# Hymba layer: value stores ahead of the inverse's loads, inverse and scan earlier in the matmul mix, second head's loads behind the scan, leading tile in mid-group

## The chip, the core and the metric

The kernel runs on one core of a Trainium2 chip. The metric is device time in microseconds (us), the median of three runs. The engines are PE (TensorE: matmuls and transposes into PSUM banks), DVE (VectorE), ACT (ScalarE), POOL (GpSimd) and SP (SyncE, which issues most DMAs, in the order of its queue).

## The reference, cut to what matters

One layer with two head groups side by side on T = 16 meta + 1024 tokens, D = 1024, all in fp32:

```
u        = rmsnorm(x);  p = u @ w_in            # one projection, split by columns
group 1: gated DeltaNet, 4 heads of 128, chunked: causal conv on q, k, v; per chunk
         solve (I + A) [U W] = rhs (A strictly lower triangular); then the scan over chunks
           v_new = U - W S;  o = (q e^g) S + (q k^T decay) v_new;  S = S e^g + k^T v_new
         o = rmsnorm(o) * w * silu(z)
group 2: forgetting attention, 8 heads of 64: logf = logsigmoid(f + b), c = cumsum(logf)
         softmax(q k^T / 8 + c_q - c_k, causal) v, in blocks of 128 queries
h   = x + concat(o1, o2) @ w_out
out = rmsnorm(h + swiglu(rmsnorm(h)))           # meta tokens dropped
```

## The kernel before, in words

**Precision.** A product in fp32 is made of three matmuls: each operand is split into a high and a low part (`split`: ACT casts the high part, DVE subtracts to get the low part, L163/L164 and L166/L167), and `mm3g` (L210) issues hi·hi, hi·lo, lo·hi. So each weight block that is loaded (`load_w`, raw_*, on SP's queue) costs one ACT and one DVE instruction (whi_*, wlo_*) before PE can use it, and each result that leaves a PSUM bank as an operand costs an ACT and a DVE instruction before the bank is free.

**What sets the order.** PE's order is written by the class `PeOrder` while the program is traced. It holds chains, which are generators that say when their next step is due, and one `fill`, a generator that is advanced by a matmul whenever no chain is due. `od.t` counts PE's time. The order on DVE, ACT, POOL and SP is set by the tile scheduler, which simulates the program; `tc.issue_after(x)` in the kernel makes an instruction wait in that order until x has been issued. Pools decide when a tile's space is free, and so which loads must wait.

**Stages around the change.** After the DeltaNet's projections:

- The *inverse* of the 64-wide triangular blocks: `invert_blocks` works on DVE (`up`, L527/L529, a chain of short instructions that begins when `ad` has been loaded, and ends with eight stores to `ud_d`, L549). Then `levels(hp)`, hp = 0, 1 for two pairs of heads, combines blocks by matmuls on PE. Each level's first step loads `ubk` (L599, 256 KB) and `na` (L601, two loads of 512 KB) on SP. They enter the mix by `od.add(levels(hp), LV0[hp] - 8.0)`, LV0 = (76, 119).
- The *fill* `fox()`: the attention's projections. First the gate z0, then values in two halves, fv1 (heads 4 to 7, with the forget gate's columns `fr`) and fv0 (heads 0 to 3), each in tiles −1 (16 meta tokens) and 0 to 7, then `fox_proj` for keys (fk) and queries (fq), four head pairs (0 to 3) in three chunks of tokens each (fq2_700 is pair 2's chunk at token 700). A value tile takes 24 matmuls. It leaves its bank by ACT, DVE and, in the first half, the copy to `fr` (L943), through `fvt`, which has three buffers, and is stored to DRAM in `v_d` (L940). A key or query chunk leaves through `fhl`, which has two buffers (ACT L768, DVE L769), and its store (L771, to `k_d` or `q_d`) is remembered in `last[0]`. `fox_load` (L710) loads the next weight block.
- After the levels the *scan* over eight chunks (L775 to L856), with `chunk_out` behind each chunk (`on` L868 on DVE, four transposes `ot` L874 on PE). The fill runs between its steps. What is left of the fill when the scan is done comes after it in one piece. Head 0's nine loads are issued in chunk 7.
- The *attention*: per head nine loads (`att_head`: `ka`, `qa`, `kk`, `sa`, `avt`), then scores (sc, L1009/L1010, sums `sm` on DVE L1014), transposes (pt), and values (po: L1075 for the meta tile by `phm` and `vm`, L1078/L1079 with the hi and lo parts `ph` and `pl`). Heads alternate between two pools: `ale` for even and `alo` for odd heads; `alo` is opened after the whole fill. `vm` holds the meta tokens' values, in eight copies of 16 rows; `vm_load` (L728) issues eight small loads per head, and head 1's call loads those of head 0 too. Head 1's loads were issued behind `last[0]`, the last store of q.
- While attention runs, its fill is the DeltaNet's half of the output projection, `wout_gdn`: tiles `wog` of 12 matmuls, each of which waits for a bank; DVE adds it to the residual `ht` (L1175), loaded from x on SP's queue while one head's loads have been issued, on POOL's queue once there are two. The fill starts `LD0` after a head's loads (10 us for the heads that lack time).
- After the heads: the attention's half of the output projection, the FFN (about half of the span) and the final norm. The change leaves them alone.

Of the kernel before, what the change touches and what calls it, by code (L numbers as in the profile page):

```python
# [9 lines left out]
F32 = mybir.dt.float32  # L10
F32R = mybir.dt.float32r
# [4 lines left out]
P = 128  # L16
# [13 lines left out]
GQ, GK, GV, GZ, FQ, FK, FV = 0, 512, 1024, 1536, 2056, 2568, 3080  # L30
TCH = ((0, 348), (348, 346), (694, 346))
GRP = 4
LV0 = (76.0, 119.0)
LAT = 0.4
ATT0 = 3.0
LEAD = 0.6
# [61 lines left out]
def tile_hymba_layer(ctx, tc, x, meta, attn_norm_w, w_in, conv_w, a_log, dt_bias, gdn_norm_w,  # L98
                     fgate_b, w_out, ffn_norm_w, w_gate, w_up, w_down, final_norm_w, out):
    nc = tc.nc  # L100
# [43 lines left out]
    rec_d = dram.tile([NT, P, 8, GH, P], F32, name="rec_d")  # L144
    ad_d = dram.tile([2, 4, 2, NT, 32, 32], F32, name="ad_d")
    ud_d = dram.tile([2, 4, 32, 2, NT, 32], F32, name="ud_d")
# [4 lines left out]
    v_d = dram.tile([FH, T, P], F32, name="v_d")  # L151
# [38 lines left out]
    def win_block(c0, n, name):  # L190
        ws = ([], [])
        for i in range(2):
            k0 = KT // 2 * i
            hl = load_w([(w_in_v[:, k0:k0 + KT // 2, c0:c0 + n], KT // 2 * n)], f"{name}_{i}")
            for o, t in zip(ws, hl):
                o.extend(t[:, n * k:n * k + n] for k in range(KT // 2))
        return ws
# [8 lines left out]
    od = PeOrder()  # L206
# [344 lines left out]
    for hp in range(2):  # L551
        c = 2 * P * hp
# [42 lines left out]
    def levels(hp):  # L595
        na = lp.tile([P, 2, NT, P], F32, tag="na", bufs=2, name=f"na_{hp}")
        tb = lp.tile([P, 2, NT, 32], F32, tag="tb", bufs=2, name=f"tb_{hp}")
        ubk = lp.tile([P, 2, NT, 32], F32, tag="ubk", bufs=2, name=f"ubk_{hp}")
        nc.sync.dma_start(ubk, ud_d[hp].rearrange("b j h t k -> (b j) h t k"))  # L599
        for i in range(2):  # L600
            nc.sync.dma_start(na[:, i], rec_d[:, :, 0, 2 * hp + i].rearrange("t p c -> p t c"))  # L601
        if not hp:
            lv_t["act"], lv_t["dve"] = tail[0]
        with tc.issue_after(lv_t["dve"].ins):
# [96 lines left out]
        yield from mm3g(acc[:rows, :n], [(uh[:, k, col:col + rows], ul[:, k, col:col + rows], w[0][k][:, :n],  # L701
                                          w[1][k][:, :n]) for k in range(KT)], n / 2400)

    last = [None]

    fox_ws = [(GZ, 256, "z0"), (FV + 256, 264, "fv1"), (FV, 256, "fv0"), (FK, 256, "fk0"), (FK + 256, 256, "fk1"),
              (FQ, 256, "fq0"), (FQ + 256, 256, "fq1")]
    fox_w = []

    def fox_load():  # L710
        if fox_ws:
            fox_w.append(win_block(*fox_ws.pop(0)))

    t_ld, hds, fixed, fq_m, h_ld = [], {}, [], [0], {}

    def att_tiles(i):
        ka = als[i].tile([NA + DH, T], F32R, name=f"ka{i}")
        qa = als[i].tile([NA + DH, S], F32R, name=f"qa{i}")
        nc.gpsimd.memset(ka[:NA].bitcast(F32), 1.0)
        nc.gpsimd.memset(qa[:NA].bitcast(F32), -1.0)  # L720
        fixed.append((ka, qa))

    NR = GRP * NM
    vms, pms = [], {}
# [194 lines left out]
    def fox():  # L919
        fox_load()  # L920
        w = fox_w.pop(0)
        for t in range(NT):
            if t == 1:
                fox_load()
            acc = ps_mm(f"z0_{t}")
            yield from proj_tmg(acc, t, w, 256)
            gate_out(t, acc, *((fvp, "fvt") if t < NT - 2 else (fp, "fhl")), 0)
        for b in (1, 0):
            n = 256 + 8 * b
            w = fox_w.pop(0)  # L930
            for t in range(-1, NT):
                if t == 1:
                    fox_load()
                col, rows = tok_cols(t)
                acc = (ps_mm if b or t % 2 else ps_t)(f"fv{b}_{t}")
                yield from proj_tmg(acc, t, w, n)
                vt = fvp.tile([P, 4, 2, DH], F32R, tag="fvt", name=f"fvt{b}_{t}")
                av = acc[:rows, :256].rearrange("p (h d) -> p h d", d=DH)
                split(vt[:rows, :, 0], vt[:rows, :, 1], av)
                nc.sync.dma_start(v_d[4 * b:4 * b + 4, col:col + rows].rearrange("h t d -> t h d"),  # L940
                                  vt[:rows].rearrange("p h a d -> p h (a d)").bitcast(F32))
                if b:
                    nc.vector.tensor_copy(fr[:rows, NT if t < 0 else t], acc[:rows, 256:264])  # L943
        fvc.close()
        yield from fox_proj(lambda m: k_d[m], TCH, 0, 1.0, "fk")
        od.add(csum(), od.t + 8.0)
        yield from fox_proj(lambda m: q_d[m].rearrange("a p c -> p a c"), ((NM, 342), (NM + 342, 342), (NM + 684, 340)), NM, -DH ** -0.5, "fq")

    lv_left, outs_left = {0, 1}, set(range(NT))
    for hp in range(2):  # L950
        od.add(levels(hp), LV0[hp] - 8.0)
    od.fill = fox()
    peo = ExitStack()
    peo.enter_context(tc.manual_schedule(engines={mybir.EngineType.PE}))
# [12 lines left out]
    od.add(scan(), od.t + 4.0, front=True)  # L967
    od.run(lambda: not outs_left)
    scc.close()
    while od.step_fill():  # L970
        pass
    uctx.close()

    alc = ExitStack()
    als.append(alc.enter_context(tc.tile_pool(name="alo", bufs=1)))
    atc = ExitStack()
    ap_ = atc.enter_context(tc.tile_pool(name="ap", bufs=1, side="right"))
    ap2 = atc.enter_context(tc.tile_pool(name="ap2", bufs=1, side="right"))
    rsum = ap_.tile([P, FH, NT], F32, name="rsum")
    for i in range(2):  # L980
        vms.append(ap2.tile([P, GRP, P], F32R, name=f"vm{i}"))
        nc.gpsimd.memset(vms[i].bitcast(F32), 0.0)
    att_tiles(1)
    masks = []

    def scores(h, g, hd, out):
# [54 lines left out]
    def values(h, g, hd, pts):  # L1041
        m, rows, vt = *hd[:2], hd[6]
        nk = GRP * (g + 1)
        nm = f"{g}_{h}"
        box = []
        for kt in (0, -1, *range(1, nk)):
            c0, j0 = NM + P * kt, max(0, kt - GRP * g)
            yield max(r for _, r in pts)
            pt = ps_t(f"pt_{nm}_{kt}")
            if kt < 0:  # L1050
                nc.tensor.transpose(pt[:NR, :P], pms.pop((h, g)), ident)
                od.pe(0.108)
            else:
                for j in range(j0, GRP):
                    nc.tensor.transpose(pt[:, P * j:P * j + P], pts[j][0][:, j, c0:c0 + P], ident)  # L1055
                    od.pe(0.108)
            q = slice(P * j0, 512)
            if kt < 0:
                ph = pl = ap2.tile([P, P], F32R, tag="phm", bufs=2, name=f"phm_{nm}")
                split(ph[:NR], ph[NR:], pt[:NR, :P])  # L1060
                meta_lo[0], meta_n[0] = tail[0][1], 0
            else:
                ph = ap2.tile([P, 512], F32R, tag="ph", bufs=3, name=f"ph_{nm}_{kt}")
                pl = ap2.tile([P, 512], F32R, tag="pl", bufs=3, name=f"pl_{nm}_{kt}")
                split(ph[:, q], pl[:, q], pt[:, q])
            nq = P if kt < 0 else 512 - P * j0
            rdy = od.on("dve", nq / 960 + 0.07, od.on("act", nq / 1200 + 0.06))

            def av(kt=kt, ph=ph, pl=pl, q=q):
                if kt == 0:  # L1070
                    box.append(ps_v(f"po_{nm}"))
                po = box[0]
                if kt < 0:
                    for j in range(GRP):
                        nc.tensor.matmul(po[:, P * j:P * j + P], vms[h % 2][:, j], ph, start=False, stop=False)  # L1075
                    od.pe(0.2135)
                    return
                nc.tensor.matmul(po[:, q], vt[:, kt], ph[:, q], start=kt == 0, stop=False)  # L1078
                nc.tensor.matmul(po[:, q], vt[:, kt], pl[:, q], start=False, stop=(kt == nk - 1))  # L1079
                od.pe((512 - q.start) / 1200)  # L1080
                if kt == nk - 1:
                    oa = ap2.tile([P, 512], F32, tag="oa", bufs=2, name=f"oa_{nm}")
                    nc.scalar.copy(oa, po)
                    od.on("act", 0.5)
                    for i in range(2):
                        last_o[0] = nc.gpsimd.dma_start(
                            o_d[GRP * g:GRP * g + GRP, rows, 4 * i + m].rearrange("t p c -> p t c"),
                            v3(oa[DH * i:DH * i + DH], GRP))

            avq.append((rdy, av))  # L1090
            yield from av_step(2)

    def attention():
        groups = [(h, g) for h in range(FH) for g in range(NT // GRP)]
        ptl, pos = {}, [0.0]

        def score_stream():
            for i, (h, g) in enumerate(groups):
                if h not in hds:
                    with tc.issue_after(last[0].ins) if h == 1 else nullcontext():  # L1100
                        hds[h] = att_head(h)
                ptl[i] = []
                for n, rdy in enumerate(scores(h, g, hds[h], ptl[i])):
                    pos[0] = i + n / (5, 9)[g]
                    yield max(rdy, t_ld[h] + LD0[i]) if i < len(LD0) else rdy
            pos[0] = 1e9

        ss = score_stream()

        def ahead(x):  # L1110
            while pos[0] < x:
                r = next(ss, None)
                if r is None:
                    return
                yield r

        yield from ahead(1.0)
        rot[0] = 0
        for i, (h, g) in enumerate(groups):
            nt = GRP * (g + 1) + 1  # L1120
            yield from ahead(i + 1.0)
            for k, rdy in enumerate(values(h, g, hds[h], ptl[i])):
                yield from ahead(i + 1.0 + LEAD + k / (2 * nt))
                yield rdy
        yield from av_step(0)
        rot[0] = 1
# [602 lines left out]
```

## Time and profile before

| | |
|---|---|
| median of 3 runs | 1305.55 us (1304.69 to 1306.87) |
| profiled execution | 1305.29 us, its span 1303.6 us, mean granted clock 0.996 |
| PE's idle time in the span, all waits | some 15 us, of which about 10 between 250 and 600 us |
| inverse's `ad` load issued | 233.03 us |
| fv1 on PE | 232.82 to 263.7 us |
| first chunk, last chunk of the scan | 375.49, 426.46 us |
| first wog tile | 439.26 us |
| attention's values | 463.5 to 590 us |

How to read it: PE is busy for nearly the whole span. A row of a timeline gives start, duration, engine, line, operation and out<-in, and in brackets how long the engine had been idle before it and what ended that. Matmuls are pipelined, so that their durations overlap; the distance between two starts is what a matmul takes of PE's time. `SPq` rows are DMA issues on SP's queue; they last as long as SP was held there.

### The profile page before, as it was taken

How to read it: one execution, taken by the hardware profiler on the slowest of the kernel's cores; microseconds unless marked ns; L12 is line 12 of the kernel's file. 1: busy time of each engine (PE TensorE's matmuls, PEld its weight loads, DVE VectorE, ACT ScalarE, POOL GpSimd, SP SyncE). 2: the span in 40 equal slices, each digit the busy share in tenths (PEclk: the TensorE clock that was granted, in tenths of full speed). 3: DMA queues.
4: the chain of work that ended last, by engine and by line, in shares of the span. 5: the costliest groups of instructions: out<-in, count | busy, mean ns of one | idle time of the engine just before them, and what ended most of it. 6: DMA issues, size and time to landing. Idle time of an engine off the chain costs nothing.

```text
span 1303.6 us, 20023 instructions
## 1 busy us (share of the span) xinstructions
PE 1281.6 (98%) x7434; PEld 1127.5 (86%) x7434; DVE 839.7 (64%) x1508; ACT 547.7 (42%) x940; POOL 348.8 (27%) x316
## 2 busy tenths in 40 slices
PE   9999999899999999999999999999999999999997
PEld 8999999899999888887778888888888888888886
DVE  6667898583246768886887666556666664365645
ACT  6455444142223557884553333233333343433332
POOL 2012213101022221112504534455334443020301
PEclk9999999999999999999999999999999999999999
DMA  6333625854389886737435644553444467945513
GB/s 230 99 118 110 183 86 141 234 143 154 127 285 304 220 236 190 183 94 253 168 114 161 198 165 155 186 163 129 159 155 166 165 212 268 393 178 197 207 64 129
DMA packets 185248, 232.07 MB, mean 178 GB/s; under 512 B 19816, under 2 KB 138176, under 8 KB 182336
## 3 DMA queue, kind: packets, MB, share of 16 engines
q1 hardware_dynamic: 182256, 222.15, 53.1%
q0 software_dynamic: 2896, 8.65, 2.2%
q8 instruction: 58, 0.95, 0.3%
q14 instruction: 38, 0.31, 0.1%
HBM read 153.11 MB, written 77.65 MB: 177 GB/s over the span
## 4 chain that ended last, share of the span: by engine, by line
PE 87%; DVE 5%; DMA 3%; issue 2%; SPq 1%; ACT 1%; POOL 0%; POOLq 0%; DVEq 0%; ACTq 0%
PE xp L1610 9%; PE yp L1610 7%; PE ua L1435 5%; PE ga L1435 5%; PE gb L1435 5%; PE ud L1435 5%; PE gd L1435 5%; PE ub L1435 5%; PE pj_fk L212 4%; PE pj_fq L212 3%; PE fv L212 3%; PE ue L1435 2%; PE ge L1435 2%; PE pt L1055 2%; PE wog L212 2%
## 5 line engine op out<-in xcount | busy, mean ns | idle before, releaser
L164 DVE TENSOR_TENSOR al_p<-ra_p,ah_p 128x2048 fp32r<-128x2048 f32 (+1 forms) x21 | 47.7, 2273 | 94.5 <-ACT ah_p L163 94.5
L163 ACT CAST ah_p<-ra_p 128x2048 fp32r<-128x2048 f32 (+1 forms) x21 | 37.1, 1767 | 106.2 <-PE xp L1610 47.9
L1610 PE MATMUL xp<-wl_p,ah_p 128*128 128x512 f32 (+1 forms) x176 | 67.3, 382 | 0.0
L1610 PE MATMUL xp<-wh_p,al_p 128*128 128x512 f32 (+1 forms) x176 | 67.3, 382 | 0.0
L1610 PE MATMUL xp<-wh_p,ah_p 128*128 128x512 f32 (+1 forms) x176 | 67.3, 382 | 0.0
L1491 POOL TENSOR_TENSOR gzw<-gzw,uzt 128x512 f32<-128x512 f32 x11 | 18.4, 1673 | 168.0 <-DVE uzt L1480 138.9
L1435 PE MATMUL gb<-uh_p,w_g_p 128*128 128x512 f32 x176 | 57.8, 389 | 0.0
L1435 PE MATMUL ub<-uh_p,w_u_p 128*128 128x512 f32 x176 | 57.7, 389 | 0.0
L1435 PE MATMUL gd<-uh_p,w_g_p 128*128 128x512 f32 x176 | 57.7, 389 | 0.0
L1435 PE MATMUL ud<-uh_p,w_u_p 128*128 128x512 f32 x176 | 57.7, 389 | 0.0
L163 ACT CAST ph<-pt 128x512 fp32r<-128x512 f32 (+1 forms) x96 | 45.2, 474 | 29.8 <-PE pt L1055 28.8
L164 DVE TENSOR_TENSOR pl<-pt,ph 128x512 fp32r<-128x512 f32 (+1 forms) x96 | 52.0, 554 | 8.4 <-ACT ph L163 7.8
L1491 POOL TENSOR_TENSOR gxy<-gxy,uxy 128x512 f32<-128x512 f32 x22 | 39.0, 1771 | 64.7 <-DVE uxy L1480 53.7
L164 DVE TENSOR_TENSOR w_u_p<-raw_u,w_u_p 128x512 fp32r<-128x512 f32 x42 | 41.9, 997 | 21.6 <-ACT w_u_p L163 21.5
L1019 ACT ACTIVATE pr<-pr,sm 128x144 f32<-128x144 f32 (+3 forms) x64 | 50.5, 791 | 10.0 <-DVE sm L1014 9.8
L1435 PE MATMUL ua<-uh_p,w_u_p 128*128 128x512 f32 x160 | 52.5, 389 | 0.0
L1435 PE MATMUL ga<-uh_p,w_g_p 128*128 128x512 f32 x160 | 52.5, 389 | 0.0
L1610 PE MATMUL yp<-wh_p,ah_p 128*128 128x512 f32 x132 | 51.3, 389 | 0.0
L1610 PE MATMUL yp<-wl_p,ah_p 128*128 128x512 f32 x132 | 51.3, 389 | 0.0
L1610 PE MATMUL yp<-wh_p,al_p 128*128 128x512 f32 x132 | 51.3, 389 | 0.0
L163 ACT CAST w_u_p<-raw_u 128x512 fp32r<-128x512 f32 x42 | 26.0, 620 | 55.7 <-PE gd L1435 36.0
L164 DVE TENSOR_TENSOR wl_p<-rw_p,wh_p 128x2048 fp32r<-128x2048 f32 (+1 forms) x21 | 46.5, 2212 | 3.8 <-ACT wh_p L163 3.8
(649 smaller groups left out, 4233.0 us busy)
## 6 DMA issues: line engine op xcount, KB each, us to landing
ra_p<-ao_p SPq DMA_DIRECT2D x14, 1024.0 KB
raw_g<-in_w_gate_dram SPq DMA_DIRECT2D x22, 512.0 KB
raw_u<-in_w_up_dram SPq DMA_DIRECT2D x22, 512.0 KB
raw_d<-in_w_down_dram SPq DMA_DIRECT2D x22, 512.0 KB
wt_p<-raw_d SPq DMA_DIRECT2D x33, 256.0 KB
rw_p<-wt_p SPq DMA_DIRECT2D x8, 1024.0 KB
rw_p<-in_w_down_dram SPq DMA_DIRECT2D x6, 1024.0 KB
ao_p<-gzw SPq DMA_DIRECT2D x22, 256.0 KB
```

The lines of the kernel that those rows point to most:

```text
L163: cast = nc.scalar.copy(dst_hi, src)
L164: low = nc.vector.tensor_sub(dst_lo, src, dst_hi.bitcast(F32))
L212: nc.tensor.matmul(dst, a, b, start=first, stop=last)
L1019: nc.scalar.activation(pr[:, :n], pr[:, :n], AF.Exp, bias=sm[:, np_ - 1:np_], scale=-1.0, accum_out=rsum[:, h, j:j + 1])
L1055: nc.tensor.transpose(pt[:, P * j:P * j + P], pts[j][0][:, j, c0:c0 + P], ident)
L1435: nc.tensor.matmul(dst, a[:, c], b[:, k], start=(first and k == 0 and i == 0), stop=(k == 3 and i == 2), skip_group_check=not first)
L1491: last_mul[0] = G.tensor_tensor(gs[d], gs[d], us[d], op=ALU.mult)
L1610: nc.tensor.matmul(dst[:, n_], a[:, f, c], b[:, f, n_], start=(first and i == 0 and n == 0), stop=(i == NF - 1 and n == 2), skip_group_che ...
```

## The change

Four parts. (1) The levels' loads are placed behind the last store of values or keys, and the weight blocks that `fox_load` fetches while no key has been stored yet are placed behind the newest value store (`vst`). (2) LV0 is lower, and the levels enter the mix 12 us earlier still; scan and all behind it come earlier in PE's order against the fill. (3) Behind the scan, ahead of what is left of the fill, `alo` is opened, `vm` and head 1's tiles are made and head 1's loads are issued; they no longer wait for the last store of q. Because head 1's loads have then been issued when `wog` begins, all loads of `ht` go to POOL's queue. (4) In groups of eight key tiles the 16-token tile −1 comes fifth, not second.

```diff
-LV0 = (76.0, 119.0)
+LV0 = (72.0, 106.0)
...
-        nc.sync.dma_start(ubk, ud_d[hp].rearrange("b j h t k -> (b j) h t k"))
-        for i in range(2):
-            nc.sync.dma_start(na[:, i], rec_d[:, :, 0, 2 * hp + i].rearrange("t p c -> p t c"))
+        with tc.issue_after((last[0] or vst[0]).ins):
+            nc.sync.dma_start(ubk, ud_d[hp].rearrange("b j h t k -> (b j) h t k"))
+            for i in range(2):
+                nc.sync.dma_start(na[:, i], rec_d[:, :, 0, 2 * hp + i].rearrange("t p c -> p t c"))
...
-    last = [None]
+    last, vst = [None], [None]
...
-            fox_w.append(win_block(*fox_ws.pop(0)))
+            with tc.issue_after(vst[0].ins) if vst[0] and not last[0] else nullcontext():
+                fox_w.append(win_block(*fox_ws.pop(0)))
...
-                nc.sync.dma_start(v_d[4 * b:4 * b + 4, col:col + rows].rearrange("h t d -> t h d"),
+                vst[0] = nc.sync.dma_start(v_d[4 * b:4 * b + 4, col:col + rows].rearrange("h t d -> t h d"),
...
-        od.add(levels(hp), LV0[hp] - 8.0)
+        od.add(levels(hp), LV0[hp] - 20.0)
...
     scc.close()
+    alc = ExitStack()
+    als.append(alc.enter_context(tc.tile_pool(name="alo", bufs=1)))
+    for i in range(2):
+        vms.append(als[1].tile([P, GRP, P], F32R, name=f"vm{i}"))
+        nc.gpsimd.memset(vms[i].bitcast(F32), 0.0)
+    att_tiles(1)
+    hds[1] = att_head(1)
     while od.step_fill():
         pass
     uctx.close()
-    alc = ExitStack()
-    als.append(alc.enter_context(tc.tile_pool(name="alo", bufs=1)))
...
-        for kt in (0, -1, *range(1, nk)):
+        for kt in (0, -1, 1, 2, 3) if nk == GRP else (0, 1, 2, 3, -1, *range(4, nk)):
...
-                    with tc.issue_after(last[0].ins) if h == 1 else nullcontext():
-                        hds[h] = att_head(h)
+                    hds[h] = att_head(h)
```

The lines behind L711 stand two further down in the changed kernel, those of the attention three. In the rows below, the number behind a name is the tile or chunk, the last one a counter.

SP's queue where the first value stores stand, before: `zt` is stored by `rec_d<-zt`, and `ubk`, `na` (the levels') and `raw_fk` (keys' weights) come ahead of `v_d<-fvt`.

```order
L307 DMA rec_d<-zt_6_2685 128x256
L599 DMA ubk_3280<-ud_d 128x512
L307 DMA rec_d<-zt_7_2713 128x256
L601 DMA na_3278<-rec_d 128x8x128
L180 DMA raw_fk_0_3056<-in_w_in_dram 128x4x256
L601 DMA na_3278<-rec_d 128x8x128
L601 DMA na_3762<-rec_d 128x8x128
L180 DMA raw_fk_1_3062<-in_w_in_dram 128x4x256
L601 DMA na_3762<-rec_d 128x8x128
L940 DMA v_d<-fvt_-1_2741 16x4x128
L940 DMA v_d<-fvt_0_2771 128x4x128
```

And now:

```order
L307 DMA rec_d<-zt_6_2685 128x256
L307 DMA rec_d<-zt_7_2713 128x256
L942 DMA v_d<-fvt_-1_2741 16x4x128
L942 DMA v_d<-fvt_0_2771 128x4x128
L180 DMA raw_fv_0_2776<-in_w_in_dram 128x4x256
L180 DMA raw_fv_1_2782<-in_w_in_dram 128x4x256
L942 DMA v_d<-fvt_1_2813 128x4x128
L942 DMA v_d<-fvt_2_2843 128x4x128
```

The five loads of the levels and the two of the keys' weights have left the place ahead of the stores; raw_fv, the weights of the second half, which stood far ahead, now stands behind the second store. (Behind these rows the other stores of the first half follow, then raw_fk, then ubk and na.)

DVE where the splits of the first half's tiles meet those weights, now: `up` is the inverse, `fvt` the low part of a value tile, `fr` the copy that frees its bank, `wlo_fv` the weights' low part.

```order
L529 TENSOR_REDUCE up_2338<-up_2338 128x8
L164 TENSOR_TENSOR wlo_fv_0_2779<-raw_fv_0_2776,whi_fv_0_2778 128x1024
L527 TENSOR_TENSOR up_2338<-up_2338,ad_2337 128x8x17
L164 TENSOR_TENSOR fvt_2_2843<-fv_2_2818,fvt_2_2843 128x4x64
L945 COPY fr<-fv_2_2818 128x8
L164 TENSOR_TENSOR wlo_fv_1_2785<-raw_fv_1_2782,whi_fv_1_2784 128x1024
```

In before, both splits stand ahead of the whole `up` chain; now they stand on either side of tile 2's.

SP's queue where head 1's loads stand, before (behind head 0's): the last two stores of q come ahead of them.

```order
L771 DMA q_d<-fhl_fq_358_4883 128x2x342
L1172 DMA ht_0_4981<-in_x_dram 128x512
L1172 DMA ht_0_5017<-in_x_dram 128x512
L1172 DMA ht_0_5096<-in_x_dram 128x512
L771 DMA q_d<-fhl_fq_700_4932 128x2x340
L737 DMA ka_4961<-c_d 3x1040
L738 DMA qa_4962<-c_d 3x1024
L741 DMA kk_5128<-k_d 64x1040
```

And now (pair 2's chunks at 358 and 700, pair 3's at 16, 358 and 700 are the last stores of q; `fhl_fq_700_4893` is fq2_700, `fhl_fq_16_4922` is fq3_16, `fhl_fq_358_4951` is fq3_358):

```order
L743 DMA kk_4865<-k_d 64x1040
L739 DMA ka_4861<-c_d 3x1040
L740 DMA qa_4862<-c_d 3x1024
L744 DMA sa_4866<-q_d 64x1024
L745 DMA ka_4861<-k_d 64x1040
L746 DMA qa_4862<-q_d 64x1024
L748 DMA avt_4875<-v_d 128x8x128
L730 DMA vm_4857<-v_d 16x128 x8
L730 DMA vm_4859<-v_d 16x128 x8
L773 DMA q_d<-fhl_fq_700_4893 128x2x340
L773 DMA q_d<-fhl_fq_16_4922 128x2x342
```

Head 1's loads have moved ahead of the stores of fq2_700 and of all of pair 3.

DVE where `wog` begins, now: `wlo_wo` are splits of the output projection's weights, `ht` drains wog's first tile, `sm` are score sums (the ISA rows), and `fhl_fq_358_4951` is the eviction of fq3_358, whose bank wog's second tile takes.

```order
L771 SCALAR_TENSOR_TENSOR fhl_fq_16_4922<-pj_fq_16_4897,fhl_fq_16_4922 128x342
L167 SCALAR_TENSOR_TENSOR wlo_wo_10_6249<-raw_wo_10_6246,gnw,whi_wo_10_6248 128x512 x2
L167 SCALAR_TENSOR_TENSOR wlo_wo_11_6257<-raw_wo_11_6254,gnw,whi_wo_11_6256 128x512 x2
L1177 TENSOR_TENSOR ht_0_5009<-wog_0_5011,ht_0_5009 128x512
L1017 ISA pr_0_5026,sm_0_0_5032<-sc_0_0_0_5033,zmask 128x144
L1017 ISA sm_0_0_5032 128x1
L1017 ISA pr_0_5026,sm_0_1_5038<-sc_0_1_0_5039,zmask 128x272
L1017 ISA sm_0_1_5038 128x1
L771 SCALAR_TENSOR_TENSOR fhl_fq_358_4951<-pj_fq_358_4926,fhl_fq_358_4951 128x342
```

In before, all evictions of fq stand ahead of the first `ht`; now the last two stand behind it.

More of the change, by code (lines that the diff above doesn't have):

```diff
@@ L979, in tile_hymba_layer @@
     rsum = ap_.tile([P, FH, NT], F32, name="rsum")
[L980 to L983, printed above, removed]
     masks = []
```

## The prediction

> **What bounds the kernel now.** I read the page's busy shares, then the waits of PE, then the timeline of each engine around the longest waits.
>
> ```profile
> span 1303.6 us, 20023 instructions
> ...
> PE 1281.6 (98%) x7434; PEld 1127.5 (86%) x7434; DVE 839.7 (64%) x1508; ACT 547.7 (42%) x940; POOL 348.8 (27%) x316
> ```
>
> PE is the bound. The change neither adds nor removes a matmul, so the time can move only by PE's waits, and by the clock while it waits. These are the waits that lie where the change works (in all, times, longest):
>
> ```profile
> PE fv L212 <- DVE fr L943: 3.3, 1, 3.3
> PE wog L212 <- DVE ht L1175: 2.4, 3, 0.8
> ...
> PE ot L874 <- DVE on L868: 1.0, 1, 1.0
> PE po L1075 <- DVE phm L164: 0.9, 1, 0.9
> ```
>
> The largest, in PE's timeline:
>
> ```profile
> 250.12 0.29 PE L212 MATMUL fv<-wlo_fv,uh 128*128 128x264 f32 x1
> 250.24 0.28 PE L212 MATMUL fv<-whi_fv,ul 128*128 128x264 f32 x1
> 253.79 0.56 PE L212 MATMUL fv<-whi_fv,uh 128*128 128x264 f32 x1 [3.27 <-DVE fr L943]
> ```
>
> Starts are 0.12 us apart before the gap. The start after it comes 3.55 us later, 3.43 more than the rhythm. Then PE runs slower for a while; the windows view has the granted clock at 0.83 over this stretch, and the second row is the first matmul back in the old rhythm:
>
> ```profile
> 250.00:255.00 5.00, 1.73 (x10) 1.55 (x9) 1.78 (x8) 1.12 (x3) 0.00 (x0) 0.83 0.71 201
> 256.77 0.28 PE L212 MATMUL fv<-wlo_fv,uh 128*128 128x264 f32 x1
> ```
>
> From 253.79 to 256.77 thirteen matmuls take 2.98 where 13 x 0.12 = 1.56: 1.4 more. The place costs 3.43 + 1.4 = **4.85 us**. [...]
>
> Why it waited, on ACT, DVE and SP's queue:
>
> ```profile
> 252.74 0.37 ACT L163 CAST fvt<-fv 128x256 fp32r<-128x256 f32 x1 [10.57 <-DMA v_d<-fvt_-1_2741]
> 253.15 0.42 DVE L164 TENSOR_TENSOR fvt<-fv,fvt 128x256 fp32r<-128x256 f32 x1 [3.95 <-ACT fvt L163]
> 243.42 2.19 SPq L180 DMA_DIRECT2D raw_fk<-in_w_in_dram  x1
> 245.65 0.83 SPq L601 DMA_DIRECT2D na<-rec_d  x1
> 246.58 1.61 SPq L940 DMA_DIRECT2D v_d<-fvt_-1_2741  x1
> ```
>
> fvt has three buffers. ACT's fourth cast waits until the first value store has landed, and that store was issued at 246.58, behind the levels' loads and the key weights.
>
> **The change part by part.** Sums are made against the profiled run: 1305.29 us, of which 1303.6 is the span; the median of the runs shown, 1305.55, is 0.26 above it.
>
> *Value stores.* In the new order the stores come straight behind the last zt store; ubk, na and raw_fk stand behind all of this half's stores. The landing thus no longer ends the wait: −4.85. New in their place: raw_fv0, the next weights, now stands behind the first two stores instead of far ahead, and on DVE its split wlo_fv_0 stands ahead of the split of fv_2, whose bank fv_5 needs (PE's turn: 250.36). The rows of these splits in before:
>
> ```profile
> L163 ACT CAST whi_fv<-raw_fv x4: 1038/1064/1076, 195.0 to 233.3; 128x1056 fp32r<-128x1056 f32 x2, 128x1024 fp32r<-128x1024 f32 x2
> L164 DVE TENSOR_TENSOR wlo_fv<-raw_fv,whi_fv x4: 1226/1238/1257, 196.3 to 234.4; 128x1056 fp32r<-128x1056 f32 x2, 128x1024 fp32r<-128x1024 f32 x2
> 245.42 0.41 DVE L164 TENSOR_TENSOR fvt<-fv,fvt 128x256 fp32r<-128x256 f32 x1
> ```
>
> The load can be issued once the second store is, at the earliest near 241, at the latest near 244.3 if DVE reaches that split as late as before. A load of 0.5 MB to landing took between about 3.5 and 6 us here (the first store: 246.58 to 252.74 on a full queue); I take 4. Then 1.05 + 1.24 + 0.41 + 0.16 (fr): the bank is free between 247.9 and 251.4, or 253 at worst. Stall: 0 to 2.6; I take 1.0, toward the late end, since DVE's chain of `up` is unchanged. Part: **−3.85**.
>
> The levels' loads, now issued later, have cover: the second half's nine tiles, 9 x 24 x 0.12 = 26 us of PE work. Without it PE would wait for na.
>
> *Scan's end.* The wait of 1.0 is that of ot_7, the scan's last transpose, and with PE's restart (0.4, as at wog below: 1.19 − 0.79) it costs 1.4. The scan now ends while fq work is left, and ot_7 stands after 24 matmuls of it, 3.8 us: **−1.4**; without that fill the wait would be back. In return DVE's gate sums (csum) fall inside the scan's first chunk: **+0.3** (0 to 1), the only place where moving the scan adds DVE work to its chain.
>
> *Head 1's loads.* Here is the new cost. In before they began after the last store of q:
>
> ```profile
> 441.37 0.29 SPq L737 DMA_DIRECT2D ka<-c_d  x1
> ...
> 446.43 0.70 SPq L746 DMA_DIRECT2D avt<-v_d  x1
> 447.23 14.49 SPq L728 DMA_DIRECT2D vm<-v_d  x16
> ```
>
> The 25 loads held SP from 441.37 to 447.23 + 14.49 = 461.72: 20.35 us, of which vm's sixteen loads of one small tile each took 14.49. Now all 25 stand ahead of the store of fq2_700, and fhl has two buffers: the eviction of fq3_358 waits until that store has landed, and wog's second tile waits for that eviction's bank. What waits on SP: kk, the first of these loads into the scan's space, waits for the scan's last `on`, and queued behind it are the store of fq2_358 and the other loads. The race: that load waits for the scan's last `on`, and these rows carry the times from there to wog's second tile:
>
> ```profile
> 430.58 0.32 PE L212 MATMUL pj_fq<-ul,whi_fq 128*128 128x342 f32 x1
> 430.74 0.32 PE L212 MATMUL pj_fq<-uh,wlo_fq 128*128 128x342 f32 x1
> 439.51 2.79 PE wog L212 x12
> 432.79 0.22 PE po L850 x2
> 437.95 0.36 DVE on L868
> 440.37 0.50 DVE L769 SCALAR_TENSOR_TENSOR fhl_fq<-pj_fq,fhl_fq 128x340 fp32r<-128x340 f32 x1
> 438.62 0.43 ACT L768 ACTIVATE fhl_fq<-pj_fq 128x340 fp32r<-128x340 f32 x1
> ```
>
> 117 fq matmuls x 0.157 = 18.4, two ot 0.8, wog 2.8, four scores 0.8: 22.8 from the last po. The last `on` followed po by 5.2, with a weight split between; I take 4.3. Lead: 18.5 us. Queue: 15 (the nine loads' 5.9, and two thirds of vm's 14.49) to 20.35, taken as 18, since wo's weights and ht, which moved beside it in before, come at other times; landing 3 (an estimate, half of the 6.2 from issue to landing above, on a queue less full); evictions 0.43 + 0.50. Stall = 18 + 3 + 0.9 − 18.5 = **+3.4**. Low end: 15 gives 0.4, but DVE's order has ht and two score sums ahead of this eviction, and in before such a pair ends late:
>
> ```profile
> 443.15 0.43 DVE L1014 CUSTOM_DVE_ANT_0 pr<-sc,zmask 128x272 f32<-128x272 f32 x1
> 442.59 0.40 PE L212 MATMUL wog<-whi_wo,uh_p 128*128 128x512 f32 x1
> ```
>
> 443.58 + 0.50 against PE's turn at 442.59 is 1.5, the floor. High end: 20.35 gives 5.8, and 7.2 with a halved clock. Whether 3.4 would halve it too is open: the one idle time of that length in this trace did; I leave the 1.4 to the range. [...]
>
> *The burst.* While head 1's loads were awaited, three wog tiles ran alone, twelve matmuls each, and each waited for the bank that ht drains:
>
> ```profile
> 453.95 0.40 PE L212 MATMUL wog<-whi_wo,ul_p 128*128 128x512 f32 x1
> 455.14 0.53 PE L212 MATMUL wog<-whi_wo,uh_p 128*128 128x512 f32 x1 [0.79 <-DVE ht L1175]
> ```
>
> 1.19 instead of 0.23, three times: −2.9. With head 1's scores offered at once, wog stands between scores and values, and ht drains beside them. It costs nothing as long as at least 0.8 us of other matmuls lie between tiles. **−2.85**. The loads of ht all go to POOL's queue now, where POOL is busy for 27% of the span: nothing. ACT and DVE get head 1's scores earlier while they still finish head 0, and wo's second set of splits moves from head 2's stretch to later heads. For both the nearest row is phm's wait of 0.9: I take half of it as lost at the start, a quarter as saved, **+0.2** (−0.9 to +0.9).
>
> *Leading tile in mid-group.* At four head starts PE waits for pl:
>
> ```profile
> 522.70 0.49 PE L1078 MATMUL po<-ph,avt 128*128 128x512 f32 x1
> 523.50 0.50 PE L1079 MATMUL po<-pl,avt 128*128 128x512 f32 x1 [0.31 <-DVE pl L164]
> ```
>
> 0.80 instead of 0.23: 4 x 0.57 = 2.3, and 1.0 where phm was late. With the narrow tile later, a wide one fills the place, and wog fill, thinned out, reaches one head further. I take half of 3.3: **−1.7** (0 to −3.3).
>
> Sum: −3.85 − 1.4 + 0.3 + 3.4 − 2.85 + 0.2 − 1.7 = **−5.9**: 1305.29 − 5.9 = **1299.4**.
>
> **The rivals.** A measurement can tell about 0.2%, 2.6 us, from no change.
>
> *The queue is quicker (0.22).* Head 1's loads fit the lead: +1.5 instead of 3.4, no wait for fv_5 (−1.0), head starts and phm at −3.0 instead of −1.7: −5.9 − 1.9 − 1.0 − 1.3 = −10.1, so 1295.2. For it: the loads are issued when nothing else of the attention's is. Against: vm's 14.49 us.
>
> *Gain eaten by the queue (0.13).* At 20.35 us and a halved clock, +7.2, with fv_5 at 2.6: −5.9 + 3.8 + 1.6 = −0.5, so 1304.8, no change. For it: that duration was measured. Against: in that stretch ht's loads and stores moved too.
>
> *Slower (0.07).* The same mechanism, beyond: behind the scan's own loads the queue waits longer still. Without this part's 3.4 the sum is −9.3, so the stall, clock included, must exceed 9.3 + 2.6 = 11.9, that is 10.5 without the clock: a queue of 18.5 + 10.5 − 3.9 = 25.1 us. At 28: stall 13.4 + 1.4, net +5.5, so 1310.8. For it: SP takes its queue in order, and two q stores stand between head 1's loads, the first of which must wait for the eviction before it. Against: no queue of this trace was that long.
>
> *The change doesn't do what it says (within the second).* Were the long fv wait only moved to the second half, 4.85 would come back: 1304.2. The second half's tiles alternate between two sets of banks, and 26 us lie ahead of the levels; both speak against it.
>
> **How the numbers follow.** Forecast 0.58, rivals 0.22, 0.13, 0.07. The forecast's own range, by the ends of the queue (1.5 to 5.8) and of fv_5 (0 to 2.6), is 1296.5 to 1303.4. Range with the rivals, leaving out the slow case and the ends: 1294.0 to 1304.5. Faster by over 0.2%: 0.58 + 0.22 + 0.01 = 0.81; within 0.2%: 0.12; slower: 0.07.
>
> **What would show it.** The 3.27 row at fv_5 should be gone, with no slow stretch behind it; a short wait behind wlo_fv instead. ot_7 and the three ht waits should be gone. The longest PE wait between 430 and 445 should be wog's second tile, behind fhl_fq, with ACT's eviction waiting for a landing of q_d. If that row is absent, or above 6 us, the forecast is wrong by that difference; so it is if the fv wait remains.

## The result, and the profile after

The changed kernel is slower: 1313.89 us (median of four runs, 1312.27 to 1316.22) against 1305.92 (1304.69 to 1306.87), ratio 1.006, 95% interval 1.0045 to 1.0074. The forecast was 1299.4 with a range up to 1304.5. The profiled execution took 1313.2 us, of which 1311.4 is the span. On its page PE has the same busy time and the same matmuls:

```profile
PE 1280.6 (98%) x7434; PEld 1128.6 (86%) x7434; DVE 839.2 (64%) x1508; ACT 546.7 (42%) x940; POOL 351.8 (27%) x319
```

A trace shows one execution, and executions of one kernel differ here by up to 6 us (e10: 1303.29 to 1309.07); those traced of e1, e8 and e12 are the longest of theirs, 2 to 4 us above the median, so that a single wait in them says less than the medians do. The 7.8 us that the span grew by are waits, and the clock (mean granted 0.992, in before 0.996). PE's waits after the change:

```profile
PE wog L212 <- DVE fhl_fq L771: 9.2, 1, 9.2
PE py L648 <- DVE u L638: 3.1, 2, 2.7
PE sc L1012 <- DVE sm L1017: 1.7, 3, 0.6
...
PE pvn L833 <- DVE r L828: 1.2, 1, 1.2
...
PE fv L212 <- DVE fr L945: 0.7, 1, 0.7
```

The old list has shrunk as forecast: fv from 3.3 to 0.7, the three waits of wog behind ht, that of ot and that of phm are gone. Two rows are new and large. One of them, wog's second tile behind fhl_fq, was forecast at 3.4 and is 9.2; the other, py at L648 behind the inverse's copy u, was not forecast at all. (The row is py2 in the kernel, the second step of the levels; I call it py2 below.)

Waits alone don't add up to the time, since the clock is lower behind the two new ones (0.58 from 300 to 308 us, 0.59 from 446 to 458). So I went through all PE rows of a trace and summed, by stretch, how much later each matmul starts after the one ahead of it than that kind of pair does in the trace of before (the median). The sums, 32.3 and 40.2, differ as the spans do:

| stretch of the span, us | before | changed | difference |
|---|---|---|---|
| value projection, 230 to 285 | 4.8 | 1.5 | −3.3 |
| inverse, 285 to 330 | 0.2 | 6.5 | +6.3 |
| scan, 330 to 430 | 5.5 | 7.5 | +2.0 |
| handover to attention, 430 to 480 | 5.8 | 11.2 | +5.4 |
| heads, 480 to 600 | 5.0 | 1.8 | −3.3 |
| all else | 11.0 | 11.7 | +0.7 |

How finely the kinds of pairs are told apart moves the differences of the handover (+5 to +11) and of the heads (−3 to −5) by some us; those of the values and the inverse hardly move (−3.3, and +6 to +7).

**The new wait in the inverse.** PE and DVE there:

```profile
296.91 0.32 PE L212 MATMUL pj_fk<-uh,whi_fk 128*128 128x346 f32 x1
299.91 0.41 PE L648 MATMUL py<-ident,u 64*64 64x64 f32 x4 [2.68 <-DVE u L638]
```

```profile
299.04 0.21 DVE L787 TENSOR_TENSOR ubm<-umt,beta 16x64 f32<-16x64 f32 x1 [5.27 <-DMA umt<-um_d]
299.18 1.39 DVE L638 COPY u<-pu 32x512 f32<-32x512 f32 x2
```

The copy that PE waits for is not late by itself. It stands on DVE behind `ubm`, which belongs to the scan's meta chunk and waits for the load of umt. That load comes late. SP's queue, of the changed kernel and then of before:

```profile
293.42 0.28 SPq L582 DMA_DIRECT2D um_d<-amt  x1
293.80 0.61 SPq L773 DMA_DIRECT2D k_d<-fhl_fk  x1
296.64 0.33 SPq L698 DMA_DIRECT2D umt<-um_d  x1
```

```profile
286.38 0.28 SPq L582 DMA_DIRECT2D um_d<-amt  x1
287.57 0.36 SPq L940 DMA_DIRECT2D v_d<-fvt  x1
287.98 0.69 SPq L697 DMA_DIRECT2D umt<-um_d  x1
```

The load is issued 8.7 us later. For 7.0 of them its data are not there: the meta chunk's inverse (`amt`) is a chain on DVE that runs between other DVE work, and it takes 17.5 us here where it took 11.0. It runs between the splits of the second half's value tiles, and one of these now waits for a store's landing, just as the first half's did before (2.1 us of DVE's time):

```profile
285.53 0.37 ACT L163 CAST fvt<-fv 128x256 fp32r<-128x256 f32 x1 [4.17 <-DMA v_d<-fvt]
285.94 0.42 DVE L164 TENSOR_TENSOR fvt<-fv,fvt 128x256 fp32r<-128x256 f32 x1 [2.12 <-ACT fvt L163]
276.35 0.48 SPq L600 DMA_DIRECT2D ubk<-ud_d  x1
276.87 1.18 SPq L602 DMA_DIRECT2D na<-rec_d  x2
278.15 4.07 SPq L942 DMA_DIRECT2D v_d<-fvt  x2
```

The inverse's loads have moved from ahead of the first half's stores to among the second half's. PE does not stop there (busy for all of 275 to 296 us), it has other banks; DVE does. The landing is not all of it: three splits of the key weights (1.2 us each), whose loads part 1 has moved behind value stores, and the levels' first instructions (1.5 us, and 0.7 of waiting for ubk) now stand inside the chain as well. And the inverse itself comes earlier: in before, py2 started at 305.27 us, here its turn was near 297.2. Both shifts together, 8.7 us of lateness and some 8 us of haste, make the wait.

**Wog's second tile.** The race that the prediction ran, on SP and ACT:

```profile
427.92 0.47 SPq L743 DMA_DIRECT2D kk<-k_d  x1
...
434.51 0.39 SPq L748 DMA_DIRECT2D avt<-v_d  x1
435.16 15.11 SPq L730 DMA_DIRECT2D vm<-v_d  x16
450.37 0.99 SPq L773 DMA_DIRECT2D q_d<-fhl_fq  x2
```

```profile
453.20 0.46 ACT L770 ACTIVATE fhl_fq<-pj_fq 128x342 fp32r<-128x342 f32 x1 [10.13 <-DMA q_d<-fhl_fq]
454.26 0.80 PE L212 MATMUL wog<-whi_wo,uh_p 128*128 128x512 f32 x1 [9.18 <-DVE fhl_fq L771]
```

The store of fq2_700 was issued at 450.37, behind all of head 1's loads, and ACT's eviction waited until it had landed. Why the queue was that long, the chain of work that ended last tells (start, length, what):

```profile
428.48 6.02 DMA q_d<-fhl_fq
434.51 11.74 DMA avt<-v_d
446.27 0.30 SPq L730
...
450.37 2.75 DMA q_d<-fhl_fq
```

`avt` goes out when the store of fq2_358, eight transfers ahead of it on SP, has landed (6.02 us), the eighth vm load when `avt`, again eight ahead, has, 11.74 us later, and the store of fq2_700 4.1 us behind that. Of the 22.4 us from kk to this store, 17.8 are these two landings. The first eight of the sixteen small loads held SP for 11.4 us, the last eight for 3.7; by SP's waits 5.4 us of the first part went to landings of larger loads ahead (`ka` 2.1, `qa` 1.5, `avt` 1.3, `sa` 0.5).

### The profile page after: what moved, and what is told of

It is laid out like the page before. It is cut to its first block, busy times and chain, and to the rows that moved or that the text cites. A ratio compares the mean times of both kernels' runs of the same rounds, so it can differ in the third digit from the quotient of the medians.

```text
span 1311.4 us, 20000 instructions
## 1 busy us (share of the span) xinstructions
PE 1280.6 (98%) x7434; PEld 1128.6 (86%) x7434; DVE 839.2 (64%) x1508; ACT 546.7 (42%) x940; POOL 351.8 (27%) x319
## 4 chain that ended last, share of the span: by engine, by line
PE 84%; DMA 7%; DVE 4%; issue 2%; ACT 1%; SPq 1%; POOL 0%; POOLq 0%; DVEq 0%; ACTq 0%
PE xp L1612 9%; PE yp L1612 7%; PE gd L1437 5%; PE ua L1437 5%; PE ga L1437 5%; PE gb L1437 5%; PE ud L1437 5%; PE ub L1437 5%; PE pj_fk L212 3%; PE pt L1058 2%; PE ge L1437 2%; PE ue L1437 2%; PE pj_fq L212 2%; PE z L212 2%; PE wog L212 2%
```

## The experiments

The kernels are compared with the kernel before; each ratio stands with its 95% interval.

**e1: ubm later.** One instruction changes its place on DVE, behind the inverse's last copies:

```diff
-        V.tensor_mul(ub, umt, beta[...])
+        with tc.issue_after(lv_t["dve"].ins):
+            V.tensor_mul(ub, umt, beta[...])
```

> The changed kernel with one instruction moved on DVE: ubm, the product of the meta chunk's inverse with beta that waits for the load of umt, stands behind the inverse's last copies instead of ahead of u<-pu. My theory: in the changed kernel PE's wait of 2.7 us at py2, with 0.4 more and a stretch of halved clock behind it, is DVE standing in ubm while umt lands, so the wait goes and the time falls by 4 to 6 us, to 1308 to 1310. Rival: u<-pu is late on its own (its matmuls or the loads of na are late), ubm only happens to stand there: the wait at py2 stays and the time stays at 1312 to 1315.

1307.53 us, ratio 1.0007 (0.9998 to 1.0016): 6.4 us less than the changed kernel. The wait at py2 is gone, the inverse's stretch is at 0.4. The rival falls: the copies were ready. In this trace part of the gain is lost at once, at pvn, the scan's first chunk, whose wait grew from 1.2 to 2.3:

```profile
PE pvn L834 <- DVE r L829: 2.3, 1, 2.3
```

In the traces of the later kernels that keep this edit (e3, e5, e9, e11) the wait is 1.3 to 1.4, so the loss may belong to the one execution.

**e2: vm later.** The sixteen small loads behind the last store of q:

```diff
-        if h:
-            for i in (0, 1) if h == 1 else (h,):
-                vm_load(i)
+        if h > 1:
+            vm_load(h)
...
     while od.step_fill():
         pass
+    for i in (0, 1):
+        with tc.issue_after(last[0].ins):
+            vm_load(i)
```

> The changed kernel with the sixteen small vm loads of heads 0 and 1 behind the last store of q; head 1's other nine loads stay early. My theory: the 9.2 us wait of wog's second tile is the store of fq2_700 standing on SP behind the vm loads (15 us), so the wait falls to 0 to 2 us, its halved clock goes, and the time falls by 8 to 11 us, to 1303 to 1306. Rival: the nine large loads fill the DMA engines, and the store lands late in any case: the wait stays above 5 us and the time above 1309. Second rival: the vm loads, now late, make the first value tile of the meta tokens wait, a new wait of 5 us or more at po L1078.

1310.23 us, ratio 1.003 (1.0019 to 1.0041): only 3.7 us less, the time of the first rival. The wait fell from 9.2 to 3.8, between theory and rival. The store is issued 15 us earlier now, at 435.24, and takes 12.5 us to land where it took 2.8. The second rival's wait did not come. **e3: both edits.**

> Both edits together. My theory: the two waits are separate in time and cause, the gains add to 13 to 17 us, 1297 to 1301, which beats the kernel before by 0.4 to 0.7%. Rival: work that is released earlier at py2 meets the next wait (the scan's start or its chunks), and only the later edit pays: 1302 to 1306.

1303.8 us, ratio 0.9982 (0.9974 to 0.9991): faster than before, but 3 us short of the theory. SP, ACT and the windows view of e3 in the handover (of a window: the granted clock, the DMA share and GB/s come last):

```profile
429.39 15.50 SPq L772 DMA_DIRECT2D q_d<-fhl_fq  x4
441.57 0.46 ACT L769 ACTIVATE fhl_fq<-pj_fq 128x342 fp32r<-128x342 f32 x1 [6.08 <-DMA q_d<-fhl_fq]
```

```profile
430.00:435.00 5.00, 5.00 (x34) 5.00 (x33) 0.10 (x1) 0.85 (x2) 0.00 (x0) 1.00 1.01 251
435.00:440.00 5.00, 4.35 (x24) 3.63 (x22) 1.32 (x2) 0.48 (x1) 1.26 (x2) 1.00 1.08 270
```

The first of these stores goes out at 429.39, and the eviction that waits for its landing starts 12.2 us later. The DMA engines are full here, with a share of 1.01 and 1.08 from 430 to 440 us: e2's first rival, the traffic, fits the rest of the wait.

**e4: part 3 taken back** (head 1's pool, tiles and loads where they were; parts 1, 2 and 4 stay).

> The changed kernel without part 3: head 1's pool, tiles and loads are where they were before, behind the last store of q; parts 1, 2 and 4 stay. My theory: the long wait of wog's second tile is gone (about -11 us with the clock), the burst of wog with its three waits is back (+2.9), and py2's wait stays: 1304 to 1307. Rival: the long wait comes from the earlier scan (part 2), after which three chunks of fq run back to back with two buffers for their results: a wait above 4 us stays at the same place and the time stays above 1309.

1307.09 us, ratio 1.0003 (0.9994 to 1.0013). The long wait is gone, the burst is back, py2's wait stays, as the theory had it; the time is at its upper end.

```profile
PE py L648 <- DVE u L638: 3.2, 2, 2.9
PE wog L212 <- DVE ht L1177: 2.4, 3, 0.8
PE po L1081 <- DVE pl L164: 2.1, 4, 0.5
```

**e5: spare buffers.** e1, and two more buffers for fq2_700 and fq3_16, so that fq3_358's eviction no longer waits for fq2_700's store:

```diff
     scc.close()
+    fp2s.append(uctx.enter_context(tc.tile_pool(name="fp2", bufs=2, side="right")))
...
-                    hl = fp.tile([P, 2, 348], F32R, tag="fhl", ...)
+                    if fp2s:
+                        nfp[0] += 1
+                    hl = (fp2s[0] if fp2s and nfp[0] < 3 else fp).tile([P, 2, 348], F32R, tag="fhl", ...)
```

> The changed kernel with ubm behind the inverse's copies (as in e1_ubm_later) and two spare buffers, in space that the scan leaves free, for the results of fq2_700 and fq3_16; head 1's 25 loads stay where the change put them, ahead of the stores. My theory: the wait of wog's second tile is only the landing of the store of fq2_700 with two buffers; with the eviction of fq3_358 free of that landing the wait falls from 8.9 us to 0 to 1.5 us, and the time to 1296 to 1300, 0.5 to 0.8% below the kernel before. Rival: the full DMA engines are what is paid for; the wait moves to another row of the same place (head 0's scores, the residual's loads, the first values), in all above 4 us, and the time stays above 1302.

1307.91 us, ratio 1.0014 (1.0005 to 1.0023): a miss. Wog's wait is gone, and one as long stands some 8 us further on:

```profile
457.38 0.39 PE L1059 MATMUL pt_-1_5133<-ident,pm 128*64 128x128 f32 x1 [9.78 <-ACT pm L1032]
457.04 0.24 ACT L1032 COPY pm<-pr 128x64 f32<-128x64 f32 x1 [13.62 <-DMA q_d<-fhl_fq]
```

ACT's copy waits for a landing of q_d again: attention's tiles take the space of the buffers for q, and that space is free only when the last stores, still behind the vm loads, have landed. So the rival holds in this form: the stores' lateness is what costs, not the two buffers.

**Parts alone: e6 (part 1), e7 (part 2), e8 (part 4)**, each applied to the kernel before.

> The kernel before with part 1 alone: the inverse's loads and the next weights behind the value stores. My theory: the wait of 3.3 us at fv_5 with its slow clock is replaced by one below 1 us, as in the changed kernel (3.3 us less in that stretch), and py2 does not wait, since the inverse stands at its old place, about 7 us later in the mix than umt's late landing: 1302 to 1304. Rival: the wait behind ubm comes from the queue alone, then it is here as well and the time is at 1306 or above.

> The kernel before with part 2 alone: inverse and scan earlier in the mix. My theory: the wait at fv_5 is still there; py2 does not wait, because umt lands early as in before; ot_7 no longer waits, the burst of wog does: 1304 to 1307, no change. Rival: the early inverse is enough by itself to make py2 wait, or the three chunks of fq left behind the scan wait for their own stores: 1308 or above.

> The kernel before with part 4 alone: the leading tile fifth in groups of eight. My theory, from the run with head 1 undone, where four head starts wait 0.53 us each for pl and the wait for phm is gone: the two cancel, 1305 to 1307, no change. Rival: as I predicted, the narrow tile in mid-group is worth 1.7 us: 1304 to 1305.

e6: 1303.88 us, ratio 0.9991 (0.9981 to 1.0002); fv waits 1.3, py2 not at all (the levels' first step, at L623, waits 0.9 for na). The theory gave another reason for that: it took umt to be as late as in the changed kernel. In e6 it is issued only 0.8 us later than in before:

```profile
288.80 0.46 SPq L698 DMA_DIRECT2D umt<-um_d  x1
```

e7: 1305.89, 0.9997 (0.9988 to 1.0006); fv waits 4.3, py2 not at all, and umt is issued at 291.15, 3.2 us later than in before. So neither part alone makes py2 wait, and neither alone makes umt that late: the chain of `amt` takes 10.3 us in e6, 11.7 in e7 and 17.5 with both. With part 1 alone the levels' loads go out behind nearly all stores of the second half (ubk at 289.78), with both among them (276.35).

e8: 1305.48, 0.9999 (0.9989 to 1.0008): part 4 removes the wait for phm and makes the four at the head starts longer:

```profile
PE po L1079 <- DVE pl L164: 2.1, 4, 0.5
```

They were five of at most 0.3.

**e9: residual later.** e3 with three of the early ht loads on SP behind the stores:

```diff
-        with tc.issue_after(ra_ld[NT - 2].ins):
-            (nc.gpsimd if len(t_ld) > 1 else nc.sync).dma_start(ht, x[cols, nbc])
+        late = not nb and 2 <= tt < 5
+        with tc.issue_after((last[0] if late else ra_ld[NT - 2]).ins):
+            (nc.sync if late else nc.gpsimd).dma_start(ht, x[cols, nbc])
```

> The kernel of e3_both (ubm and vm later) with three of the five early loads of the residual ht, 0.75 MB, moved from POOL's queue to SP's, behind the last store of q and the vm loads. My theory: in e3_both the store of fq2_700 is issued as soon as its data are there and still takes 6 us to land, because the DMA engines are full with head 1's loads, the stores and the five ht loads; 0.75 MB less at some 255 GB/s lands it 2 to 3 us earlier, wog's wait falls from 3.3 to below 1.5 us without a slow clock, and the time to 1300 to 1302. Rival: the landing hangs on the store's own rows or on the queue's order and not on the traffic: the wait stays at 3 us or more and the time at 1303 to 1305.

1303.31 us, ratio 0.9972 (0.9961 to 0.9983). Wog's wait is 0.5, as the theory said, but the time hardly fell and is the rival's: sc, a few matmuls further on, waits 3.3 behind the DVE work that is now due there.

```profile
PE sc L1015 <- DVE sm L1020: 5.0, 4, 3.3
...
PE wog L212 <- DVE fhl_fq L770: 0.5, 1, 0.5
```

It is the same landing still. The store of fq2_700, issued at 429.42, takes 9.5 us until ACT's eviction starts (not the 6 us that the theory took for e3, which are ACT's idle time, but 12.2 there), and what ACT and DVE could not do meanwhile, splits of wo's weights above all, comes ahead of the score sums:

```profile
438.96 0.46 ACT L769 ACTIVATE fhl_fq<-pj_fq 128x342 fp32r<-128x342 f32 x1 [9.64 <-DMA q_d<-fhl_fq]
440.06 2.74 DVE L167 SCALAR_TENSOR_TENSOR wlo_wo<-raw_wo,gnw,whi_wo 128x512 fp32r<-128x512 f32 x4
```

**e10: part 2 taken back** (parts 1, 3 and 4 stay), and **e12**, the same with the first three loads of ht on ACT's queue:

```diff
-            (nc.gpsimd if len(t_ld) > 1 else nc.sync).dma_start(ht, x[cols, nbc])
+            (nc.scalar if not nb and tt < 3 else nc.gpsimd).dma_start(ht, x[cols, nbc])
```

> The changed kernel without part 2: inverse and scan at their old places in the mix; parts 1, 3 and 4 as in the change. My theory: with the scan at its old place the last stores of q stand ahead of the vm loads on SP and all of fq's matmuls are done before wog begins, so the long wait is gone; umt lands before the inverse needs it, so py2's wait is gone; the short wait at fv_5 and the even spread of wog stay: 1298 to 1301, below the kernel before. Rival: head 1's loads, issued only after the scan's end some 12 us later than now, are too late for scores that come at once: waits of 4 us or more at sc or at the first values, 1304 or above.

> The kernel of e10_part2_undone with the first three residual loads ht on ACT's queue instead of POOL's, where they stand behind the memsets of vm, ka and qa and are issued at 440.3 us, after wog's first tile has begun. My theory: e10's wait of 4.9 us at sc is DVE standing in the first ht, whose load came late by POOL's queue; issued 3 us earlier it costs 2 us or less and does not slow the clock, and the time falls from 1305.1 to 1301 to 1303. Rival: the load lands late because head 1's loads fill the DMA engines, whichever queue it is issued on: the wait stays at 4 us or more and the time at 1304 to 1306.

e10: 1305.09 us, ratio 0.9989 (0.9979 to 0.9998). Wog and py2 don't wait, but sc waits 4.9, a wait and a time like the rival's, though not behind head 1's loads: DVE stands in the first ht, whose load POOL issued at 440.27 and which by the trace landed at 448.05:

```profile
448.13 0.69 DVE L1177 TENSOR_TENSOR ht<-wog,ht 128x512 f32<-128x512 f32 x1 [5.23 <-issue]
440.27 2.95 POOL L1174 DMA_DIRECT2D ht<-in_x_dram  x5
```

e12: 1305.71 us, ratio 0.9994 (0.9984 to 1.0005). Issued at 441.2 on ACT, the load is there when it is needed (the ht row is at 444.32, idle before it 0.85 <-PE). In this trace all of it lies 3.7 us later than in e10's, so the issue is 2.8 us earlier against PE's work. The time is unchanged: the wait has moved to head 1's own data.

```profile
PE po L1078 <- DMA vm<-v_d: 2.4, 1, 2.4
PE sc L1012 <- DVE sm L1017: 1.7, 3, 0.6
```

Neither theory nor rival of e12 is right as put: the load's place on POOL was e10's wait, and, as far as this one trace shows, the traffic (DMA share 0.94 and 1.06 from 445 to 455 us) took the gain back.

**e11: part 3 taken back, ubm later** (e4 with e1's edit).

> The changed kernel without part 3 (as in e4_head1_undone) and with ubm behind the inverse's copies. My theory: both long waits are gone, the burst of wog is there: e4's 1307.1 less 6: 1300 to 1302. Rival: the earlier scan meets its first chunk's loads or a store of q, as in e1_ubm_later where the wait at pvn grew from 1.2 to 2.3 us, and gives half of it back: 1303 to 1305.

1301.28 us, ratio 0.9958 (0.9946 to 0.9971): the lowest median here, some 5 us below before (4 to 7 by the interval, which overlaps e9's). The theory holds. Its stretches: values 1.8, inverse 0.4, scan 7.3, handover 2.8, heads 5.7. It keeps parts 1, 2 and 4 of the change.

## Why the prediction was wrong, point by point

**The sum.** The forecast was −5.9 us; it came to +7.8 in the span. The two large errors are the inverse (+6.3, not in the sum) and head 1's loads (9.2 us of wait for 3.4).

**Value stores: right.** The wait at fv_5 is 0.7 (forecast 1.0) and stands behind the split that was named:

```profile
249.47 1.23 DVE L164 TENSOR_TENSOR wlo_fv<-raw_fv,whi_fv 128x1024 fp32r<-128x1024 f32 x1 [1.57 <-ACT whi_fv L163]
...
250.83 0.42 DVE L164 TENSOR_TENSOR fvt<-fv,fvt 128x256 fp32r<-128x256 f32 x1
251.16 0.15 DVE L945 COPY fr<-fv 128x8 f32<-128x8 f32 x1
```

The bank is free at 251.31; the forecast had 247.9 to 251.4. With 0.35 of wait at an earlier tile the stretch gained 3.3, forecast 3.85.

**The levels' cover: the step that failed.** The prediction gave the inverse's later loads "cover: the second half's nine tiles" and looked only whether na would be late. It was not. What the loads met there it put at nothing, without a look at DVE: the second half's stores land late and hold ACT's casts, these hold DVE, the key weights' splits come late as well, and DVE's queue carries the meta chunk's inverse, whose result stands ahead of the inverse's copies. The rival that let the long wait move to the second half (1304.2, inside the second case) named the right place, but looked at PE's banks there. e1 shows that ubm's place on DVE turns this into PE's wait; e6 and e7 show that it needs part 1 and part 2 together; the lateness of umt does too. Its price, 6.3, is twice the wait, since the clock fell to 0.58 behind it.

**Head 1's loads: right wait, queue mis-sized.** The row that was named as the sign came, and above the 6 us that were to count against the forecast. Forecast: queue 18 + landing 3 + evictions 0.9 − lead 18.5 = 3.4. Measured: from kk at 427.92 to the store's issue at 450.37 22.4; to ACT's start at 453.20 2.8; to PE's start 1.1; PE's turn was 454.26 − 9.18 = 445.08, a lead of 17.2. 22.4 + 2.8 + 1.1 − 17.2 = 9.1. The error is the queue. I took less than the one duration that the trace showed, 20.35, "since wo's weights and ht come at other times", and made that duration the upper bound. The opposite came: five loads of ht were issued in the same window, by POOL, and two stores of q stood among the loads. And the row of 14.49 us was misread: in before too vm's issues stood and waited for landings of head 1's larger loads (5.5 us in all by SP's waits; the first eight issues took 10.9 us, the last eight 3.6), so it was in good part no price of sixteen small issues but one of the traffic. The DMA share tells it, of after (then of before, quoted here from the window that held head 1's loads):

```profile
430.00:435.00 5.00, 5.00 (x35) 5.00 (x33) 1.17 (x2) 1.33 (x3) 3.64 (x6) 1.00 1.04 267
```

```profile
447.00:462.00 15.00, 12.89 (x60) 9.49 (x58) 7.68 (x23) 5.80 (x13) 2.22 (x5) 1.00 0.88 216
```

So "the loads of ht all go to POOL's queue now: nothing" failed as well. By e9, loads issued by POOL slowed a store issued by SP: 0.75 MB less from POOL brought the landing of an SP store from 12.2 to 9.5 us and wog's wait behind it from 3.3 to 0.5. That the traffic, more than the order of one queue, is the limit of this window is what e2, e3 and e9 point to: with the store issued some 15 us earlier, its landing took 12.5, 12.2 and 9.5 us instead of 2.8. In e5, e10 and e12 too another transfer was late when one was moved out of the way, but there an issue's place on SP or POOL came in as well.

**The clock.** I left the price of a halved clock out of the likeliest case. It came at both new waits: 0.58 from 300 to 308 us (0.50 from 302 on) and 0.59 from 446 to 458 (0.50 from 450 on), in the latter mostly while PE waited anyway.

**The scan: right in its end, wrong in its start.** ot_7 no longer waits. But pvn waits 1.2 for r, which stands on DVE behind an eviction of fq, and this one too waits for a landing, that of a key chunk's store:

```profile
365.51 0.46 ACT L770 ACTIVATE fhl_fq<-pj_fq 128x342 fp32r<-128x342 f32 x1 [2.93 <-DMA k_d<-fhl_fk]
```

csum's 0.3 was not it. The scan's stretch lost 2.0 where −1.4 + 0.3 was forecast for scan and ot_7 together (ot_7 itself lies in the next stretch).

**The burst: right.** Its three waits are gone in every run with part 3 and there in every run without it (e6 has two of the three); what it gave, the handover took back.

**The leading tile: wrong in cause.** Part 4 alone gives nothing (e8). The heads' stretch did gain 3.3 in the changed kernel, but most of that belongs to part 3, whose wog fill reaches two head starts further: with part 3 taken back the stretch is at 4.1 (e4) and 5.7 (e11).

**The other side.** The rival that ended slower needed a queue above 25.1 us; at 22.4 it did not decide alone. With the heads' and the burst's gains the handover's loss would have come out near 1307 (e1); the inverse made the rest.

## What to carry to other kernels

When loads are moved behind other transfers on a queue, follow whose landing each of those transfers gates, engine by engine, until the next in-order queue is clean; a free bank for PE says nothing about the engine that empties it (here DVE stood for 2.1 us where PE did not wait). A queue's length measured once (20.35 us here, then 22.4) is no upper bound when the change also puts other engines' transfers into the same window: ask first which landings the issues waited for, and add up the bytes of the window. And an instruction that waits for a load should stand behind the work that does not need it, as ubm in e1, where one changed place was worth 6 us.

## What the runs showed of the hardware

In before, the wait of 3.27 us was followed by a granted clock of 0.51 from 253.7 to 256.8 us. In the changed kernel shorter waits were followed by a longer stretch. The 2.68 and 0.40 us at py2 came ahead of

```profile
300.00:308.00 8.00, 7.60 (x62) 6.71 (x64) 1.09 (x2) 1.16 (x2) 0.00 (x0) 0.58 0.13 46
```

a clock of 0.58 over 8 us (0.82 from 300 to 302, 0.50 from 302 to 308), which is 8 x 0.42 x 2 = 6.7 us at the 0.50, twice the 3.4 us around the wait of 3.27 (0.83 over the ten us from 250). In e1 the 2.3 us at pvn came with a clock of 0.88 from 358 to 372 us; in e3, with a wait of 1.4 at pvn, the clock of that window is 1.00. It also came with no wait of PE in the view: in e2 it is 0.88 from 358 to 372 us, where PE is busy for all of the 14 us. What decides it is not settled by these runs.

The sixteen vm loads of 8 KB each held SP for 9.0 us in e3 (mean DMA share 0.40 and 0.39 from 445 to 455 us) and 8.4 in e9 (0.37 and 0.25 from 440 to 450), and for 14.5 us in before (share 0.88), 15.1 in the changed kernel (0.80) and 16.4 in e10 (1.01 and 1.07 from 445 to 455 us): in these runs the same small loads held SP longer beside more traffic. By SP's waits, 5.5 of the 14.5 us in before and 5.4 of the 15.1 in the changed kernel went to landings of the larger loads ahead.
